# A hybrid Mamba-2/MLA trunk kernel: a planner that groups the scan's products of neighbouring chunks and knows the array's mode changes, x loaded in column halves, merged transposes, and more staged slices of the gated output

## The chip, the cores and the metric

The kernel runs on one core of a Trainium2 chip. A core has a matrix engine (TensorE, PE in the profile, with its weight loads as PEld), a vector engine (VectorE, DVE), a scalar engine (ScalarE, ACT), a general engine (GpSimd, POOL) and a sync engine (SyncE, SP) that here issues nearly all DMAs. Each engine takes its own instructions strictly in the order in which the program lists them. Engines wait for each other by semaphores. The metric is the device time of one launch in microseconds (us).

## What is computed

The reference is a trunk of two layers on x of 2048 tokens by 1024 features, all in float32: a Mamba-2 mixer, then multi-head latent attention (MLA), each behind an RMSNorm and with a residual add, and a last RMSNorm.

```python
def mamba2_mixer(h, w_in, conv_w, conv_b, dt_bias, A_log, D_skip, g_out, w_out):
    proj = h @ w_in                                  # z, x B C, dt
    xBC = silu(causal_depthwise_conv(xBC, conv_w, conv_b))
    dt = softplus(dt_raw + dt_bias)
    y = ssd_chunked_scan(xh, dt, A, B, C)            # 32 heads of 64, 4 groups, state 128
    y = (y + D_skip * xh) * silu(z)
    y = group_rms(y) * g_out                         # 4 groups of 512 channels
    return y @ w_out

def step(state, inp):                                # one chunk of the scan
    y_intra = einsum(C B^T, L, dt, x)                # L = exp(cum_t - cum_s), causal
    y_inter = einsum(C, state, exp(cum))
    new_state = state * exp(cum_end) + einsum(B, w_end, x)

def mla_shared_kv(h, ...):                           # 256 latents + 32 rotary
    ckv = rms_norm(rms_norm(h) @ w_dkv)
    kv = ckv @ w_ukv                                 # k and v of 16 heads of 64

def mla_mixer(h, k_nope, k_rope, v, ...):
    cq, gate = split(h @ w_in)                       # 384 latents, 1024 gates
    q = rms_norm(cq) @ w_uq
    o = causal_block_attention(q, k, v)              # 16 heads, 2048 tokens
    return (o * silu(gate)) @ w_out
```

The output is `rms_norm(h, g_final)` after both residuals.

## The kernel before

**Stages.** The 2048 tokens are four blocks b of 512, each kept as four row tiles of 128 by 1024. The stages and their stretches in the profiled execution are: the layers part, which holds Mamba (to about 1400 us) and the MLA projections (to about 1930 us); the attention (to about 2600 us); and `back()`, the output projection with the final norm (to the end).

**Mamba.** There are 16 items (b, g): a token block and one of the four groups of heads. For each item `xbc` and `zgate` make the projections of a group (products of the split weights `wsp` with the transposed x, `xT`), `ssd` runs the scan, and `outp` projects the gated result back. The loop in `mamba` (L1448) interleaves the scan of one item with the projections of the next. Most products are three passes over split operands (a high and a low half).

A block begins with `load_x` (L1547: four loads of 128 by 1024 floats, the tiles `hx`, and the rows' mean squares on ACT, written into `yt`), then `prep`, which transposes the tiles on PE into `ps` banks and splits each bank into the high half of `xT` on ACT and the low half on DVE, and `steps`, which works out dt and its running sums in small tiles named `big` and `d_dt` on DVE. The constants lie in one tile, `pack`: an identity matrix in its first 128 columns, then masks and vectors.

**The scan of a chunk.** An item has four chunks c of 128 tokens, so there are 64 in all. `decays` (L1798) loads the row of running sums broadcast into a tile `big` of 128 by 8 by 128 (ring of two buffers), and turns it on ACT (eight Relu of 128 by 128, one Exp of 128 by 1024) and DVE (a product with the tile `CB`) into the decay matrix E. `inputs` makes `Xd` (x times dt) and others. In `ssd` (L1847) the chunk's inner product is 16 matmuls, for eight heads and two halves of the chunk, each with 64 output rows and 64 columns, into the bank `yi`:

```python
for h in range(8):
    hc = slice(h * 64, (h + 1) * 64)
    for t in (slice(0, 64), slice(64, P)):
        nc.tensor.matmul(yi[t, hc], E[:, h, t], Xd[:, hc], start=True, stop=True)
```

Nearly all other matmuls of the layers part use 128 output rows. In the profile each of these 16 leaves two records (`ps<-Xd,big 128*64 128x64`), so 32 records to a chunk.

**Who sets the order.** In the layers part no engine is called directly. The class `Score` (L523) records every instruction with the buffers it uses. `cost` (L570) gives each an issue time and a latency in ns, `graph` (L630) works out who must wait for whom, and `plan` (L832) repeats two passes PLANS times: `forward` (L698) is a list scheduler that simulates the five engines and the DMA and always takes the ready instruction of highest rank, and `backward` (L780) gives new ranks as the time left to the end; rings of buffers are handed out in the order in which their tiles started. The best of the plans is kept and `play` (L875) writes it out, so every instruction of the layers part carries the line L878.

**MLA.** `mla_kv_down` and `mla_cq` make the latents; `turned` (L2062) scales each of four row tiles, splits it into a float16 pair and transposes it with DMAs on SP: one DMA for each row tile and each 128 latents, so 8 for the keys' latents and 12 for the queries' in a block. The results `yT` and `BC` are the operands of the up-projections.

**Attention.** Its order comes from the class `Pace`, a simulation of its own with fixed tables. Within it, slices k of block 0's gated output are staged for `back()`: task G loads the attention's output, the gate and a row of scales into a staging tile `os` (L2251, L2254), H multiplies them (L2260, L2262), I and J split the product into a float16 pair (L2324, L2327). GATED is the number of staging tiles, and ASKED says behind which of the last heads each slice is asked for.

**back().** For each block, 8 slices k are the contraction of the output projection: `gated` (L2459) loads the three parts into `os` (three buffers), gates them on DVE, makes the high half `oT` on ACT (L2466) and the low half on DVE (L2467), and PE adds the three products into eight banks. `residual` (L2479) adds the banks into the row tiles `h`; `final` (L2483) norms them on DVE (L2487) and stores them. This part is ordered by the tile framework, close to the order of the code.

## Time and profile before

The profile is one execution; the other figures are device times of runs of the kernel.

| what | us |
| --- | --- |
| median of 3 runs | 2784.39 |
| lowest and highest of the runs | 2779.01 and 2787.86 |
| the profiled execution's own time | 2791.74 |
| its span, first to last instruction | 2789.9 |
| time around the span | 1.8 |
| mean granted TensorE clock | 0.994 |

A row of the windows view gives a stretch, the busy time and the count of instructions of each engine in it, the granted clock as a share of full speed, the share of the DMA engines' time, and GB/s. A row of the lines view is a group of instructions: its line, engine and operation, the tiles out<-in, the shapes (for matmuls first the rows of the stationary operand by its columns), the count, the busy time and the mean of one in ns, and the engine's idle time just ahead of them with what ended it. A row of the timeline has the start, the length, the engine and the operation, and in brackets the idle time before it and what ended that. Busy times of two engines overlap, so they do not add up to the span. The kernel before has its layers part on L878; the changed kernel has it on L907.

### The profile page before, as it was taken

How to read it: one execution, taken by the hardware profiler on the slowest of the kernel's cores; microseconds unless marked ns; L12 is line 12 of the kernel's file. 1: busy time of each engine (PE TensorE's matmuls, PEld its weight loads, DVE VectorE, ACT ScalarE, POOL GpSimd, SP SyncE). 2: the span in 40 equal slices, each digit the busy share in tenths (PEclk: the TensorE clock that was granted, in tenths of full speed). 3: DMA queues.
4: the chain of work that ended last, by engine and by line, in shares of the span. 5: the costliest groups of instructions: out<-in, count | busy, mean ns of one | idle time of the engine just before them, and what ended most of it. 6: DMA issues, size and time to landing. Idle time of an engine off the chain costs nothing. (4 is left out here: it accounts for less than half of the span.)

```text
span 2789.9 us, 48569 instructions
## 1 busy us (share of the span) xinstructions
PE 2737.9 (98%) x16120; PEld 1550.7 (56%) x16120; DVE 2220.0 (80%) x5048; ACT 1864.2 (67%) x4914; POOL 675.6 (24%) x832
## 2 busy tenths in 40 slices
PE   7999999999999999999999999999999999999998
PEld 6888766554555555555555545454555555555443
DVE  5889899999988879888786564646889888889676
ACT  6889877877776667666655453334888888888322
POOL 0000000000000000000002121324888888888200
PEclk9999999999999999999999999999999999999999
DMA  5333456768668655586567987976999999999894
GB/s 178 98 113 105 118 178 220 215 204 256 187 187 256 175 141 178 160 243 185 145 186 232 292 236 210 250 197 183 181 189 183 186 203 198 190 200 185 209 278 153
DMA packets 687904, 535.88 MB, mean 192 GB/s; under 512 B 496642, under 2 KB 538626, under 8 KB 687652
## 3 DMA queue, kind: packets, MB, share of 16 engines
q1 hardware_dynamic: 674500, 490.16, 69.4%
q0 software_dynamic: 13152, 42.61, 5.1%
q8 instruction: 127, 2.08, 0.3%
q14 instruction: 125, 1.02, 0.1%
HBM read 307.57 MB, written 108.66 MB: 149 GB/s over the span
## 5 line engine op out<-in xcount | busy, mean ns | idle before, releaser
L878 PE MATMUL ps<-xT,wsp 128*128 128x512 f16 (+2 forms) x2416 | 567.7, 386 | 8.7 <-DVE wsp L878 6.0
L878 PE MATMUL ps<-wsp,xT 128*128 128x512 f16 (+3 forms) x2304 | 464.4, 358 | 1.9 <-DVE Sp L878 1.2
L2356 ACT ACTIVATE Pr<-ps,nm 128x512 f32<-128x512 f32 (+3 forms) x640 | 394.5, 628 | 83.7 <-DVE nm L2351 78.1
L2345 DVE TENSOR_REDUCE mx<-ps 128x1 f32<-128x512 f32 (+3 forms) x640 | 366.4, 604 | 54.1 <-PE ps L2311 45.9
L878 PEld LDWEIGHTS <-wsp 128*128 128x128 f16 x2448 | 234.0, 98 | 281.2 <-issue 21.6
L2362 POOL TENSOR_TENSOR HL<-Pr,HL 128x512 f16<-128x512 f32 x320 | 372.6, 1164 | 25.6
L878 PE MATMUL ps<-wsp,yT 128*128 128x512 f16 (+1 forms) x1536 | 356.7, 385 | 1.0 <-DVE rb L878 0.6
L878 POOL DMA_DIRECT2D gate_d<-xs x24 | 13.8, 590 | 1115.4 <-DVE kn L878 1101.3
L878 PEld LDWEIGHTS <-xT 128*128 128x128 f16 x1920 | 185.7, 98 | 166.5 <-issue 6.2
L904 PE MATMUL ps<-K,xT 96*128 96x512 f16 (+3 forms) x640 | 223.0, 348 | 2.9 <-ACT Pr L2356 1.8
L906 PE MATMUL ps<-K,xT 96*128 96x512 f16 (+3 forms) x640 | 221.9, 347 | 0.0
L905 PE MATMUL ps<-K,xT 96*128 96x512 f16 (+3 forms) x640 | 221.8, 347 | 0.0
L2361 POOL CAST HL<-Pr 128x512 f16<-128x512 f32 x320 | 196.6, 614 | 91.7 <-ACT Pr L2356 91.5
L878 DVE SCALAR_TENSOR_TENSOR cacc<-craw,pack,cacc 128x512 f32<-128x512 f32 x288 | 211.4, 746 | 4.6 <-ACT cacc L878 4.1
L878 PEld LDWEIGHTS <-yT 128*128 128x128 f16 x1152 | 110.2, 98 | 129.2 <-issue 3.8
L878 ACT ACTIVATE big<-big,d_cum 128x128 f32<-128x128 f32 x512 | 168.5, 393 | 8.8 <-DMA big<-cumT 8.8
L878 PE MATMUL ps<-xT,st 128*128 128x512 f16 x672 | 154.8, 382 | 3.7 <-DMA st<-w_d 3.7
L2375 ACT ACTIVATE PH<-ps 128x512 f16<-128x512 f32 (+3 forms) x320 | 143.4, 484 | 14.1 <-PE ps L2370 13.3
L2397 PE MATMUL ps<-PX,xT 128*64 128x512 f16 (+1 forms) x640 | 146.2, 383 | 1.6 <-DMA PX<-HL 1.2
L2397 PEld LDWEIGHTS <-xT 128*128 128x128 f16 (+1 forms) x1280 | 95.4, 103 | 91.4 <-issue 15.4
L2356 ACT ACTIVATION_READ_ACCUMULATOR Pr<-ps,nm 128x1 f32 x640 | 133.8, 209 | 0.0
L2370 PE MATMUL ps<-pack,Pr 128*128 128x128 f32 x896 | 133.4, 274 | 0.3 <-ACT Pr L2356 0.3
(380 smaller groups left out, 5348.3 us busy)
## 6 DMA issues: line engine op xcount, KB each, us to landing
wsp<-w_d SPq DMA_DIRECT2D x68, 512.0 KB, 3.9
wraw<-in_ssm_w_in_dram SPq DMA_DIRECT2D x128, 256.0 KB, 3.2
big<-cumT SPq DMA_DIRECT2D x64, 512.0 KB, 4.2
wraw<-in_ssm_w_out_dram SPq DMA_DIRECT2D x64, 256.0 KB, 3.3
w_d<-wsp SPq DMA_DIRECT2D x32, 512.0 KB, 4.3
wsp<-wo_d SPq DMA_DIRECT2D x32, 512.0 KB, 4.3
st<-w_d SPq DMA_DIRECT2D x56, 256.0 KB, 3.7
wsp<-wu_d SPq DMA_DIRECT2D x28, 512.0 KB, 4.2
```

Source lines behind the costliest of these rows:

```text
L878: call(*[self.real(x) for x in args], **{k: self.real(x) for k, x in named.items()})
L904: mm(out, l_hi, r_hi, start=start, stop=False)
L905: mm(out, l_hi, r_lo, start=False, stop=False)
L906: mm(out, l_lo, r_hi, start=False, stop=stop)
L2345: v.tensor_reduce(m[:, at:at + 1], s, AX.X, ALU.max, negate=True)
L2356: nc.scalar.activation(tile("Pr", n, j, c)[:, :w], bank("S", n, j, c)[:, :w], AF.Exp, bias=moves[(4 * n + j) % len(moves)], accum_out=sums ...
L2361: nc.gpsimd.tensor_copy(u[:, 0], x)
L2362: nc.gpsimd.tensor_tensor(u[:, 1], x, u[:, 0], ALU.subtract)
L2370: nc.tensor.transpose(bank("T", n, k)[:, j * P:(j + 1) * P], tile("Pr", n, j, k // 4)[:, k % 4 * P:(k % 4 + 1) * P], self.ident)
L2375: nc.scalar.activation(tile("PH", n, k)[:, c], bank("T", n, k)[:, c], AF.Copy)
L2397: nc.tensor.matmul(o, weights, half(n, k, low), start=start, stop=not left[n][at[0]])
```

## The change

It has six parts.

1. The planner's model: DMAs get an issue time, a latency and a time on the wires (`wires`); an SP instruction may not be planned more than EARLY (30 us) ahead of its due time; PLANS goes from 12 to 16; a matmul with 64 output rows and at least 64 columns belongs to `half`, a change between `half` and the rest costs TURN (119 or 94 ns) in `forward`, and PE stays among the `half` ones while one is ready.
2. Pairs: `parts` names the 16 matmuls of each chunk. The first chunk's 16 of a pair (c = 0 or 2) also get the second chunk's needs from other engines, and both banks keep neighbouring places in the ring, so that both groups can be planned as one of 32.
3. The start: `pack` is loaded in two DMAs, the identity first; x of block 0 in column halves, eight loads in place of four; `links` put the first four half loads ahead of the rest of `pack` and the four square passes on ACT behind the fourth split of `xT`.
4. `turned`: one DMA for up to 256 latents, so 4 in place of 8 and 8 in place of 12 in a block.
5. The staging of gated slices in the attention: four sets in place of two (two of them in places whose tiles are done with), another ASKED, and a delay of 7500 in place of 5500 ns in the simulation.
6. `back()`: five buffers of `os` in place of three.

```diff
-GATED = 2
-ASKED = {61: (0,), 62: (1,), 63: (2, 3, 4, 5, 6)}
+GATED = 4
+ASKED = {62: (0, 1), 63: (2, 3, 4, 5, 6)}
...
-                self.at(self.now + 5500, lambda k: self.ready["DVE"].append(("H", k, 0)), k)
+                self.at(self.now + 7500, lambda k: self.ready["DVE"].append(("H", k, 0)), k)
...
-PLANS = 12
+PLANS = 16
+EARLY = 30000
...
             if named.get("transpose"):
-                return 1400, 3300
-            issue = 700 if engine == "POOL" else 400
-            return issue, -moved
+                self.wires[len(self.ops)] = 545 + moved / 288
+                return 1300, 2470 + moved / 276
+            self.wires[len(self.ops)] = 102 + moved / 359
+            return 700 if engine == "POOL" else 400, 2000 + moved / 276
...
+            if out.shape[0] == 64 and n >= 64:
+                self.half.add(len(self.ops))
...
+        for m, n in self.links:
+            if all(m != k for k, _ in preds[n]):
+                preds[n].append((m, False))
+        for (b, g, c), part in self.parts.items():
+            if c % 2 == 0:
+                needs = {m for n in self.parts[b, g, c + 1] for m, _ in preds[n] if ops[m][0] != "PE"}
+                for n in part:
+                    preds[n] += [(m, True) for m in needs]
...
+    TURN = 119, 94
...
-        est = [0.0] * len(ops)
+        est = [max(0.0, due + rank[n] - EARLY) if o[0] == "SP" else 0.0 for n, o in enumerate(ops)]
...
-                heapq.heappush(r, (rank[n], n))
+                heapq.heappush(ready["half"] if n in self.half else r, (rank[n], n))
+            if e == "PE" and ready["half"] and (mode or not r or ready["half"][0] < r[0]):
+                r = ready["half"]
...
+            if e == "PE" and mode != (n in self.half):
+                mode = not mode
+                t += self.TURN[mode]
...
-                order = sorted(self.owns, key=lambda o: (min(start[n] for n in o.ops), o.first))
+                at = {id(o): (min(start[n] for n in o.ops), o.first) for o in self.owns}
+                for (b, g, c), part in self.parts.items():
+                    if c % 2:
+                        pair = [ops[x[0]][4][0].own for x in (self.parts[b, g, c - 1], part)]
+                        at[id(pair[1])] = at[id(pair[0])]
+                order = sorted(self.owns, key=lambda o: at[id(o)])
...
-        nc.sync.dma_start(self.pack, self.a["c_pack"])
+        for cs in (slice(0, P), slice(P, PACK)):
+            nc.sync.dma_start(self.pack[:, cs], self.a["c_pack"][:, cs])
+        ops = self.score.ops
         self.load_x(0, self.a["x"][0:TB])
+        self.score.links += [(0, n) for n in range(2, 6)] + [(n, 1) for n in range(2, 6)]
+        squares = [n for n, o in enumerate(ops) if o[0] == "ACT"][:4]
...
+            if n == 0:
+                turned = [n for n in range(at, len(ops)) if ops[n][0] == "ACT"]
+                self.score.links += [(turned[3], n) for n in squares]
...
-        for i in range(4):
-            nc.sync.dma_start(xs[i], src[i * P:(i + 1) * P, :])
+        n = 1 if b else 2
+        for h in range(n):
+            cs = slice(h * D // n, (h + 1) * D // n)
+            for i in range(4):
+                nc.sync.dma_start(xs[i][:, cs], src[i * P:(i + 1) * P, cs])
...
+            self.score.parts[b, g, c] = range(at, len(self.score.ops))
...
-            for k in range(n):
-                nc.sync.dma_start(out[k][:, i], u[:, k].rearrange("p s c -> p (s c)"), transpose=True)
+            for k, m, o in sets:
+                nc.sync.dma_start(o[:, i], u[:, k:k + m].rearrange("p k s c -> p (k s c)"), transpose=True)
...
-            self.staged = [self.t(self.wo, f"os{k}", [P, 3, TB], bufs=1) for k in range(GATED)]
+            staged = [self.t(self.wo, f"os{k}", [P, 3, TB], bufs=1) for k in range(2)]
...
+            self.staged = staged + [free[0:3], free[4:7]]
...
-                s = self.t(sp, "os", [P, 3, TB], bufs=3)
+                s = self.t(sp, "os", [P, 3, TB], bufs=5)
```

How the instructions move at three places follows; a row is an instruction, or several alike, as the program lists them for one engine, and a number behind a tile's name tells buffers apart.

On PE, at the first two chunks of item (0, 3), before: the bank of the first chunk is `ps_3893`, written by products of `Xd` and `big`.

```order
L878 MATMUL ps_3851<-xT_3677,wraw_3834 64x512
L878 MATMUL ps_3847<-wsp_3740,yT_3792 128x512 x2
L878 MATMUL ps_3893<-Xd_3766,big_3349 64x64 x12
L878 MATMUL ps_3909<-pack,yt_3891 128x128 x4
L878 MATMUL ps_3893<-Xd_3766,big_3349 64x64 x4
L878 MATMUL ps_3925<-Xp_3828,Bt_3614 128x512 x2
L878 MATMUL ps_3818<-wsp_3756,yT_3680 128x512
```

The same place in the changed kernel; the banks of the two chunks are `ps_4446` and `ps_4471`.

```order
L907 LDWEIGHTS wsp_4259
L907 MATMUL ps_4371<-xT_3683,wsp_4259 128x512
L907 MATMUL ps_4446<-Xd_3759,big_3779 64x64 x16
L907 MATMUL ps_4471<-Xd_4059,big_4344 64x64 x16
L907 MATMUL ps_4496<-Sp_4251,Ct_3770 128x512 x3
L907 MATMUL ps_4505<-pack,xs_3274 128x128
L907 MATMUL ps_4505<-pack,xs_3377 128x128
```

Two runs of 12 and 4, with the next chunk's products elsewhere, have become one run of 32. Over the layers part PE changes between matmuls of 64 and of 128 output rows 164 times before and 78 times now, so it goes into the 64-row mode and back 82 and 39 times; the number of matmuls is the same, and in the attention it is 96 changes in both.

On ACT at the start of the program, before: the squares of the four x tiles are the writes of `yt` and `ms`, and `wsp` is the first split weight, that of dt.

```order
L878 ACTIVATE pack<-pack 128x32
L878 ACTIVATE yt_171,ms_172<-hx_139 128x1024
L878 ACTIVATE yt_191,ms_172<-hx_148 128x1024
L878 ACTIVATE yt_208,ms_172<-hx_150 128x1024
L878 ACTIVATE yt_216,ms_172<-hx_152 128x1024
L878 ACTIVATE xT_230<-ps_174,pack 128x512
L878 ACTIVATE xT_240<-ps_176,pack 128x512
L878 ACTIVATE wsp_243<-wraw_154 128x8x32
```

The same place in the changed kernel; `wsp_227` is the first split weight of B and C.

```order
L907 ACTIVATE xT_187<-ps_162,pack 128x512
L907 ACTIVATE xT_193<-ps_164,pack 128x512
L907 ACTIVATE wsp_196<-wraw_155 128x8x32
L907 ACTIVATE pack<-pack 128x32
L907 ACTIVATE xT_187<-ps_166,pack 128x512
L907 ACTIVATE xT_193<-ps_168,pack 128x512
L907 ACTIVATE yt_220,ms_221<-hx_139 128x1024
L907 ACTIVATE wsp_227,nrm<-wraw_160 128x256
```

Four splits of `xT` and the first weight now stand ahead of the first square pass, and weight splits stand between the square passes. On SP, eight loads of 512 KB (four `hs`, four `hx` of the next block), which stood between the third and the fourth weight load, now stand behind many more weights, and the second halves of x stand among the first weights; on DVE, the dt chain, about 20 instructions on `big`, stood ahead of the weight splits and is now mixed with them.

On DVE in `back()`, at the turn from block 0 to block 1, before: `oT_29928` and `oT_29938` are the low halves of the seventh and eighth slice of block 1, and the writes of `h` are block 0's final norm.

```order
L2467 TENSOR_TENSOR oT_29877<-os_29870,oT_29877 128x512
L1338 SCALAR_TENSOR_TENSOR rsy_4128_29911<-rsq_4127_29909,rsy_4125_29905 128x4
L2487 SCALAR_TENSOR_TENSOR h_29804<-h_29804,rsy_4128_29911,gf 128x1024
L2487 SCALAR_TENSOR_TENSOR h_29805<-h_29805,rsy_4128_29911,gf 128x1024
L2487 SCALAR_TENSOR_TENSOR h_29806<-h_29806,rsy_4128_29911,gf 128x1024
L2487 SCALAR_TENSOR_TENSOR h_29807<-h_29807,rsy_4128_29911,gf 128x1024
L2260 TENSOR_TENSOR os_29921<-os_29921 128x512
L2260 TENSOR_TENSOR os_29931<-os_29931 128x512
L2262 SCALAR_TENSOR_TENSOR os_29921<-os_29921,us 128x512
L2262 SCALAR_TENSOR_TENSOR os_29931<-os_29931,us 128x512
L2467 TENSOR_TENSOR oT_29928<-os_29921,oT_29928 128x512
L2467 TENSOR_TENSOR oT_29938<-os_29931,oT_29938 128x512
```

The same place in the changed kernel; `oT_29903` is the eighth slice of block 1, and `os_30118` is the first of block 2.

```order
L2303 TENSOR_TENSOR os_29896<-os_29896 128x512
L1365 SCALAR_TENSOR_TENSOR rsq_4119_29874<-rsx_4109_29854,rss_4118_29872 128x4
L2305 SCALAR_TENSOR_TENSOR os_29896<-os_29896,us 128x512
L1367 SCALAR_TENSOR_TENSOR rsy_4120_29876<-rsq_4119_29874,rsy_4117_29870 128x4
L2534 SCALAR_TENSOR_TENSOR h_29769<-h_29769,rsy_4120_29876,gf 128x1024
L2534 SCALAR_TENSOR_TENSOR h_29770<-h_29770,rsy_4120_29876,gf 128x1024
L2534 SCALAR_TENSOR_TENSOR h_29771<-h_29771,rsy_4120_29876,gf 128x1024
L2534 SCALAR_TENSOR_TENSOR h_29772<-h_29772,rsy_4120_29876,gf 128x1024
L2514 TENSOR_TENSOR oT_29903<-os_29896,oT_29903 128x512
L2303 TENSOR_TENSOR os_30118<-os_30118 128x512
L2305 SCALAR_TENSOR_TENSOR os_30118<-os_30118,us 128x512
L2514 TENSOR_TENSOR oT_30125<-os_30118,oT_30125 128x512
```

Before, the gating of the seventh and eighth slice stood behind the four writes of `h`; now the seventh stands wholly ahead of them, and of the eighth only the low half, one instruction, stands behind.

More of the change, by code (lines that the diff above doesn't have):

```diff
@@ L525, in __init__ @@
     def __init__(self, nc, blank, name):
-        self.ops, self.owns, self.rings = [], [], {}
+        self.ops, self.owns, self.rings, self.wires, self.links = [], [], {}, {}, []
+        self.half, self.parts = set(), {}
         self.blank, self.name = blank, name
@@ L705, in forward @@
         waiting = {e: [] for e in ENGINES}
-        ready = {e: [] for e in ENGINES}
+        ready = {e: [] for e in ENGINES + ("half",)}
+        mode = False
         events = [(0.0, e) for e in ENGINES]
@@ L760, in forward @@
                 free[e] = t + step
-            if took < 0:
-                dma = max(dma, t) - took / 260
-                took = max(dma, t + 1900 - took / 160) - t + self.LATE
+            if n in self.wires:
+                dma = max(dma, t + 500) + self.wires[n]
+                took = max(took, dma + 1690 - t) + self.LATE
             if e == "SP":
@@ L838, in plan @@
         order = sorted(self.owns, key=lambda o: o.first)
-        best = None
+        best, due = None, 0.0
         for i in range(PLANS):
-            made = self.forward(rank, order)
+            made = self.forward(rank, order, due)
             if made is None:
@@ L2060, in latent, with turned @@
         return raw, f
-    def turned(self, raw, f, n, tag):
+    def turned(self, raw, f, n):
         nc = self.nc
-        out = [self.t(self.sp, tag, [P, 4, 2, P], F16, bufs=4) for _ in range(n)]
+        sets = [(k, m, self.t(self.sp, "yT" if m == 2 else "BC", [P, 4, 2 * m, P], F16, bufs=4))
+                for k, m in ((0, 2), (2, 1))[:n - 1]]
         for i, x in enumerate(raw):
```

37 lines of the change are left out of this document (23 added, 14 removed).

## The prediction

> **What bounds the kernel now.** I read the page's busy times first, then the windows by stage, then PE's lines and timeline in the stages where it idles.
>
> ```profile
> span 2789.9 us, 48569 instructions
> PE 2737.9 (98%) x16120; PEld 1550.7 (56%) x16120; DVE 2220.0 (80%) x5048; ACT 1864.2 (67%) x4914; POOL 675.6 (24%) x832
> 0.00:70.00 70.00, 54.66 (x230) 42.41 (x230) 39.44 (x105) 44.33 (x119) 0.20 (x4) 0.93 0.55 179
> 70.00:1400.00 1330.00, 1329.40 (x7998) 780.22 (x7997) 1159.85 (x2486) 975.73 (x2569) 0.70 (x1) 1.00 0.62 177
> 1400.00:1930.00 530.00, 516.24 (x2757) 263.58 (x2756) 305.22 (x704) 234.38 (x467) 115.88 (x170) 0.99 0.79 226
> 1930.00:2600.00 670.00, 664.83 (x4338) 386.68 (x4337) 594.09 (x1521) 566.35 (x1680) 551.70 (x652) 1.00 1.01 189
> 2600.00:2790.00 190.00, 172.81 (x806) 77.85 (x804) 121.37 (x236) 43.38 (x82) 7.07 (x7) 0.97 0.73 216
> ```
>
> PE is the bound: 52 of 2789.9 us are idle. Its idle time by stage is 70 − 54.66 = 15.3 at the start, 0.6 in the whole scan, 13.8 in the MLA projections, 5.2 in the attention and 17.2 in the tail, of which some is the work behind the last matmul. So time can go in two ways: from idle and half-clock time outside the scan, or, within the scan, from what the array itself takes, since there no wait is left to remove.
>
> **Changes of the array's mode (part 2, with the planner).** This is PE's timeline around one chunk's products:
>
> ```profile
> 414.63 1.89 PE L878 MATMUL ps<-xT,wsp 128*128 128x512 f16 x8
> 416.36 0.27 PE L878 MATMUL ps<-pack,BC 128*128 128x128 f32 x1
> ...
> 416.79 1.03 PE L878 MATMUL ps<-Xd,big 128*64 128x64 f32 x28
> 417.75 0.82 PE L878 MATMUL ps<-wsp,xT 128*128 128x512 f16 x3
> 418.50 0.34 PE L878 MATMUL ps<-Xd,big 128*64 128x64 f32 x4
> 418.77 0.39 PE L878 MATMUL ps<-wsp,xT 128*128 128x512 f16 x1
> ```
>
> From start to next start, 28 records took 417.75 − 416.79 = 0.96, and 4 records 418.77 − 418.50 = 0.27, with the same kind of product behind. So a record costs (0.96 − 0.27)/24 = 0.029, and a stay that returns at once costs 0.27 − 4 × 0.029 = 0.155 more than its records. The entry shows ahead of it: a product of 512 columns takes (416.36 − 414.63)/8 = 0.216, three take 0.65, and from 417.75 to 418.50 passed 0.75, so 0.10. A stay therefore costs about 0.26. The order has 82 stays before and 39 now, 43 fewer: 43 × 0.26 = 11. It is one place in the trace; the lower bound takes the entry alone, 4.4, the upper the 0.26 with a little more, 12. PE was busy 1329.40 of 1330 there, so I know of no idle time in which this could already be hidden. I take −11.
>
> **New waits in the scan (pairs, EARLY, other ranks).** A pair needs the inputs of two chunks at once, and PE takes its work in order, so a late E of the second chunk stops everything queued behind: the state products and the projections. The planner knows all of this only from its model, and the model's DMA and latency figures change in the same edit. Bounds: 0, as the 0.6 of idle shows what planned waits cost before, and 20, since the same planner leaves 13.8 in MLA's 530 us, at which rate the scan would idle 35, and a little over half of that is the most that I give to an edit of the ranks. I take +4, nearer the scan's own row. The one reason for a gain is better ranks, and with 0.6 of idle there is none to gain.
>
> **The start (part 3).** PE, ACT and the loads:
>
> ```profile
> 5.63 1.09 PE L878 MATMUL ps<-pack,hx 128*128 128x128 f32 x4 [5.63 <-DMA hx<-in_x_dram]
> ...
> 15.01 1.07 PE L878 MATMUL ps<-xT,wsp 128*64 128x512 f32 x3 [1.89 <-DVE wsp L878]
> ...
> 25.84 0.96 PE L878 MATMUL ps<-xT,wsp 128*128 128x512 f32 x3 [0.88 <-ACT wsp L878]
> 30.91 6.07 PE L878 MATMUL ps<-xT,wsp 128*128 128x512 f32 x15 [4.10 <-DVE wsp L878]
> ...
> 43.56 22.66 PE L878 MATMUL ps<-xT,wsp 128*128 128x512 f32 x96 [1.69 <-ACT wsp L878]
> ```
>
> ```profile
> 12.40 1.27 ACT L878 ACTIVATE xT<-ps,pack 128x512 fp32r<-128x512 f32 x2 [0.69 <-PE ps L878]
> ```
>
> ```profile
> L878 ACT ACTIVATE xT<-ps,pack 128x512 fp32r<-128x512 f32 x8 | 5.0, 702 | 0.7 <-PE ps L878 0.7
> L878 ACT ACTIVATE wsp<-wraw 128x256 fp32r<-128x256 f32 x13 | 5.0, 421 | 5.9 <-DMA wraw<-in_ssm_w_in_dram 5.9
> L878 ACT ACTIVATE yt<-hx 128x1024 bf16<-128x1024 f32 x4 | 4.2, 1057 | 2.6 <-DMA hx<-in_x_dram 2.6
> ```
>
> ```profile
> wraw<-in_ssm_w_in_dram SPq DMA_DIRECT2D x128, 256.0 KB, 3.2
> hx<-in_x_dram SPq DMA_DIRECT2D x16, 512.0 KB, 5.2
> ```
>
> ```profile
> 15.50:19.00 3.50, 3.34 (x9) 1.68 (x8) 3.50 (x8) 3.35 (x10) 0.00 (x0) 0.51 1.02 408
> 29.20:36.00 6.80, 5.09 (x12) 4.07 (x13) 3.97 (x15) 0.82 (x3) 0.00 (x0) 0.50 0.31 71
> ```
>
> The stage has 15.3 of idle and two stretches at half clock, which cost 0.49 × 3.34 + 0.50 × 5.09 = 4.2 more: 19.5. Three things go. A half of a tile (256 KB) lands in about 3.2 where a whole one takes 5.2; since the queue is shared I take 1.2 of the 2.0. The first split of `xT` at 12.40 waits behind the four squares (4.2); they now stand later. The waits of 0.88, 4.10 and 1.69 are for split weights that were queued behind other loads and behind the dt chain on DVE. What sets the pace then is ACT: 5.0 for xT, 4.2 for the squares, and 16 weight passes and their sums at about 0.5 each, 8: some 17 us from about 6.5, so the last weight is split near 25, where PE waited for the last one until 43.56. The first load still takes 4.4 of the 19.5, so at most 15 goes; at least 5 goes, if only the two middle waits (0.88 + 4.10) do. ACT keeps short gaps and the dt chain is itself later, so I take −12, nearer the upper end because the order shows all three moves. What is passed: five more DMAs on SP, and the loads of the next block move behind the weights; they are wanted only a block later, about 330 us on, so nothing is late for that.
>
> The Trainium skill, page "DMA: Bandwidth & Descriptors", section Bandwidth, says to batch DMAs to 1 MiB and more for 75% of peak, which speaks against halving 512 KB loads; the two rows (256 KB in 3.2, 512 KB in 5.2) agree that a byte costs more in the smaller one, and only the first landing counts here. [...]
>
> The half clock in 15.5 to 19.0 came behind an idle time of only 1.89, that in 29.2 to 36.0 behind one of 4.10. The Trainium skill, page "TensorE: Matmul & The Clock Gate", Part 1, has the clock fall after at least one idle window of about 3.4 us; the second row agrees and the first doesn't. By the page only the 2.5 us of the second would go with the waits, and the start's term would be −10.
>
> **MLA (part 4, and the planner).**
>
> ```profile
> 1568.60:1572.00 3.40, 3.40 (x9) 1.19 (x9) 3.40 (x7) 0.69 (x2) 2.65 (x4) 0.50 1.02 333
> 1800.70:1807.50 6.80, 5.82 (x14) 2.09 (x15) 6.10 (x13) 1.38 (x2) 2.02 (x4) 0.50 0.89 268
> ```
>
> ```profile
> L878 PE MATMUL ps<-xT,st 128*128 128x512 f16 x670 | 154.4, 382 | 3.7 <-DMA st<-w_d 3.7
> ...
> L878 PE MATMUL ps<-yT,wsp 128*128 128x512 f16 x432 | 101.3, 386 | 7.8 <-DVE yT L878 4.5 <-DVE big L878 2.7 <-DVE Xp L878 0.7
> ```
>
> ```profile
> 1554.49 10.62 SPq L878 DMA_TRANSPOSE xT<-wsp  x4
> ```
>
> ```profile
> 1565.55 0.88 DVE L878 TENSOR_SCALAR xT<-xT,xg 128x1024 f16<-128x1024 f16 x2 [5.80 <-DMA xT<-wsp]
> ```
>
> Of the idle 13.8, 3.7 is for a load and 4.5 for DVE, which itself sat 5.80 for a transpose; the two half-clock stretches cost (3.40 + 5.82)/2 = 4.6. So 18 is there. SP spent 10.62/4 = 2.7 on a transpose there; 32 of its transposes go, but the bytes stay, and the one that DVE waited for at 1565.55 isn't among them. In the order that rescaling stands 10 places behind the last weight split in place of 5, and one such pass takes 0.88/2 = 0.44, so 5 × 0.44 = 2.2 more is covered. I take −6: the 2.2, the half-clock stretch that follows the wait (3.40/2 = 1.7), and 2 of the 8 of idle that DVE and the load hold, from a plan that now counts a transpose's time on the wires. Bounds: −16, all but a remnant, and +6, if the new plan has another such wait as at 1565.55.
>
> **Attention and the tail (parts 5 and 6).**
>
> ```profile
> L904 PE MATMUL ps<-W,oT 128*128 128x512 f16 x192 | 73.5, 383 | 5.9 <-ACT oT L2466 5.9
> ...
> L906 PE MATMUL ps<-W,xT 128*128 128x512 f16 x16 | 6.1, 380 | 2.0 <-DVE xT L2327 2.0
> ```
>
> ```profile
> 2660.72 4.87 DVE L2487 SCALAR_TENSOR_TENSOR h<-h,rsy,gf 128x1024 f32<-128x1024 f32 x4
> ```
>
> ```profile
> 2667.49 1.29 ACT L2466 ACTIVATE oT<-os 128x512 f16<-128x512 f32 x2 [7.68 <-DVE os L2262]
> ```
>
> The 5.9 is PE's wait for `oT`, whose gating stands behind DVE's four norm passes (4.87): ACT sat 7.68 for it. With five `os` buffers the seventh slice is gated ahead of those passes, and of the eighth only the low half is behind. The 2.0 at the stage's start is for a staged slice; with four sets the slices are made earlier. So 7.9 is there; some comes back, as the eighth's low half still waits for up to 4.87, while the products of the seventh (24 of 0.216, 5.2) cover it. I take −5, bounds −2 (the staged slice alone) and −8 (all). In the attention, where PE is busy 664.83 of 670, the second asking one head earlier moves six SP loads and a few DVE passes; DVE's 594.09 of 670 hides them, and if it didn't they would cost a few tenths each.
>
> **The sum.** −11 + 4 − 12 − 6 − 5 = −30. Against the profiled execution, 2791.74 becomes 2762. That execution lies 7.4 above the median of the runs; the terms are differences, so from the median 2784.4 the forecast is **2754**.
>
> **The rivals.** *Pairs wait (slower).* The ring `big` has two buffers, and a pair holds both until its last product; then both E of the next pair must be loaded and made.
>
> ```profile
> big<-cumT SPq DMA_DIRECT2D x64, 512.0 KB, 4.2
> ```
>
> ```profile
> L878 ACT ACTIVATE big<-big,d_cum 128x128 f32<-128x128 f32 x512 | 168.5, 393 | 8.8 <-DMA big<-cumT 8.8
> ...
> L878 ACT ACTIVATE big<-big 128x1024 f32<-128x1024 f32 (+1 forms) x68 | 68.7, 1010 | 1.6 <-DVE big L878 1.4
> ```
>
> ```profile
> L878 DVE TENSOR_TENSOR big<-big,CB 128x1024 f32<-128x1024 f32 x64 | 77.9, 1219 | 0.9 <-ACT big L878 0.5
> ```
>
> That chain is 4.2 + 2 × (168.5/64 + 1.01) + 1.2 = 12.7, if nothing else stands between. A pair comes every 1330/32 = 41.6, so there are 29 to spare, and that is what speaks against it; for it, that ACT is busy 73% and DVE 87% there, so the chain is much longer than its own work. It decides from a mean wait of (2793 − 2750)/31 = 1.4 at each of 31 pairs; with 2 the time is 2754 − 4 + 62 = 2812. *DVE takes the bound.* With 1159.85 of 1330 busy, PE's gain in the scan runs into DVE's order: the 11 is given back as waits and the other terms stay, −12 − 6 − 5 and 8 of new waits: 2769. *MLA's waits all go*, −16 in place of −6: 2744. *The halves bring nothing*: eight loads end as late as four, the weights behind them too, and only the two middle waits go, −5 in place of −12 at the start: 2761. *The change does not do what it says:* the array's turn is no cost of its own, only what the next weight load takes anyway (0 in place of −11), the start brings 5, the tail 2, and MLA's new plan loses 6: 2787.
>
> **How the numbers follow.** Forecast 0.52; DVE 0.18; MLA 0.09; halves 0.09; nothing gained 0.08; pairs wait 0.04. A difference of 0.3%, 8.4 us, is about what a measurement of this kernel tells from no change: faster is below 2776, slower above 2793. The first four are faster, 0.88; the fifth the same, 0.08; the last slower, 0.04. The range reaches below to the forecast with MLA at its end and the start at 15 and a little more, 2754 − 10 − 3 − 5 = 2736, and above to the DVE rival with the start at its lower bound, 2769 + 5 = 2774; about 0.15 lies outside.
>
> **What would show it.** Right: the stretch of the scan shorter by 7 to 12 with PE's idle there under 8; records of `Xd,big` in runs of 64; the last wait for `wsp` before 35; the 5.9 at `oT` under 2. Wrong: idle at `Xd,big` released by `big` on DVE or ACT (pairs wait); PE's idle in the scan up by 10 spread over products released by DVE; PE's busy time in the scan unchanged with 43 stays fewer, which would end the mode's price; a new MLA wait of several us. A time above 2776 would make the prediction wrong.

## The result and the profile after

The changed kernel took 2742.93 us (median of 4 runs, 2740.09 to 2749.07), the kernel before 2785.11 beside it (2779.01 to 2787.86): a ratio of 0.985, 95% interval 0.983 to 0.987, so 42 us less. The forecast was 2754 with a range of 2736 to 2774. The two profiled executions lie further apart than the medians, 2789.9 − 2738.2 = 51.7 in their spans, since the one of before is 6.6 above its kernel's median and the one of after 2.8 below; the parts below are parts of the 51.7. Four executions, one each of `oldcost` and `plans28` below and two of the kernel before beside them, took 4028 to 4446 us at a granted clock of 0.59 to 0.65, and no ratio here counts them.

The page of the changed kernel, its first lines, and its windows up to 1930 us:

```profile
span 2738.2 us, 48514 instructions
PE 2710.9 (99%) x16120; PEld 1543.6 (56%) x16120; DVE 2212.3 (81%) x5048; ACT 1867.2 (68%) x4914; POOL 672.3 (25%) x832
```

```profile
0.00:70.00 70.00, 63.48 (x287) 50.24 (x288) 49.76 (x127) 53.99 (x147) 0.20 (x4) 1.00 0.49 137
70.00:1400.00 1330.00, 1329.27 (x8117) 781.53 (x8116) 1167.34 (x2523) 988.84 (x2595) 0.70 (x1) 1.00 0.63 182
1400.00:1930.00 530.00, 526.16 (x2852) 272.80 (x2850) 320.61 (x754) 252.15 (x525) 149.13 (x212) 1.00 0.84 235
```

PE's idle time fell from 52.0 to 27.3. In the first 70 us it is 6.5 where it was 15.3, in the scan 0.7 (it was 0.6), and in the 530 us that held the MLA projections 3.8 (it was 13.8). The granted clock is 1.00 in all three, where it was 0.93 and 0.99 in the first and the third.

Where the time went is seen from when the same work is reached. These are rows of the tile view, with the shortest, median and longest time in ns and the first and last start of a group; of before:

```profile
L878 PE MATMUL ps<-Xd,big x2048: 222/222/271, 92.1 to 1447.2; 128*64 128x64 f32 x187
L904 PE MATMUL ps<-K,xT x640: 218/378/631, 1930.6 to 2593.7; 96*128 96x512 f16 x128, 96*128 96x128 f16 x16, 96*128 96x384 f16 x16
L904 PE MATMUL ps<-W,oT x192: 379/379/634, 2648.4 to 2780.2; 128*128 128x512 f16 x192
```

and of after:

```profile
L907 PE MATMUL ps<-Xd,big x2048: 222/222/271, 82.2 to 1416.1; 128*64 128x64 f32 x187
L933 PE MATMUL ps<-K,xT x640: 219/378/390, 1887.6 to 2549.2; 96*128 96x512 f16 x128, 96*128 96x128 f16 x16, 96*128 96x384 f16 x16
L933 PE MATMUL ps<-W,oT x192: 379/379/379, 2605.1 to 2728.7; 128*128 128x512 f16 x192
```

The last product of the scan comes 31.1 earlier, the first of the attention 43.0, the last of the attention 44.5, the last of the output projection 51.5. So the start and the scan gained about 31, MLA 12, the attention 1.5 and the tail 7.

**The start.** From PE's timeline in the first 75 us, and ACT's first split:

```profile
3.96 1.08 PE L907 MATMUL ps<-pack,hx 128*128 128x128 f32 x4 [3.96 <-DMA hx<-in_x_dram]
...
9.46 0.66 PE L907 MATMUL ps<-pack,hx 128*128 128x128 f32 x4 [1.17 <-DMA hx<-in_x_dram]
...
18.60 4.45 PE L907 MATMUL ps<-xT,wsp 128*128 128x512 f32 x18 [0.75 <-ACT wsp L907]
...
24.75 22.18 PE L907 MATMUL ps<-xT,wsp 128*128 128x512 f32 x94
```

```profile
7.99 1.26 ACT L907 ACTIVATE xT<-ps,pack 128x512 fp32r<-128x512 f32 x2 [5.56 <-PE ps L907]
```

The first half of x is there 1.7 earlier, the first split 4.4 earlier, and after 18.60 PE waits for no weight; before, the last such wait ended at 43.56. Idle fell by 8.8, and the 4.2 of half clock are gone: 13.0.

**The scan.** A pair in the timeline:

```profile
406.64 2.09 PE L907 MATMUL ps<-Xd,big 128*64 128x64 f32 x64
408.65 2.98 PE L907 MATMUL ps<-wsp,xT 128*128 128x512 f16 x13
```

64 records, two chunks, in one stay of 2.01 from start to start, with no idle time ahead. Over the whole kernel the lines view has it so:

```profile
L907 PE MATMUL ps<-Xd,big 128*64 128x64 f32 x2048 | 66.9, 224 | 0.0
```

**MLA and the tail.** The waits for `yT` (4.46 at 1568.52) and for `st` (3.67 at 1801.68) have no counterpart; what is left is 1.86 and 0.68 for `BC`. In the tail PE never waits for `oT`: the longest of those products takes 379 ns where it was 634, so the half clock has gone as well. From the first of them to the last it is 123.6 where it was 131.8, so 8.2 less. Ahead of the first of them 1.2 was lost: PE now waits 2.40 for `PL` at 2558.46 and 1.63 for `PX` at 2565.13, while its 2.03 for `xT` at 2607.91 has gone.

### The profile page after: what moved, and what is told of

It reads as the page before. It is cut to its first block, busy times and chain, and to the rows that moved or that the text cites. A ratio compares the mean times of both kernels' runs of the same rounds, so it can differ in the third digit from the quotient of the medians.

```text
span 2738.2 us, 48514 instructions
## 1 busy us (share of the span) xinstructions
PE 2710.9 (99%) x16120; PEld 1543.6 (56%) x16120; DVE 2212.3 (81%) x5048; ACT 1867.2 (68%) x4914; POOL 672.3 (25%) x832
## 4 chain that ended last, share of the span: by engine, by line
PE 92%; DMA 3%; DVE 2%; ACT 1%; issue 1%; SPq 0%; POOL 0%; DVEq 0%; ACTq 0%
PE ps L907 64%; PE ps L2444 6%; PE ps L933 6%; PE ps L934 6%; PE ps L935 6%; PE ps L2417 3%; DMA xT<-wsp 1%; DVE mx L2392 1%; PE ps L2359 0%; DMA PX<-HL 0%; DMA h_d<-hs 0%; DMA yT<-yt 0%; DMA hs<-h_d 0%; ACT wsp L907 0%; DMA xT<-ri_d 0%
## 5 line engine op out<-in xcount | busy, mean ns | idle before, releaser
L907 PE MATMUL ps<-xT,wsp 128*128 128x512 f16 (+2 forms) x2416 | 559.9, 384 | 0.7 <-ACT wsp L907 0.7
L907 PE MATMUL ps<-wsp,yT 128*128 128x512 f16 (+1 forms) x1728 | 398.2, 384 | 0.0
L907 PEld LDWEIGHTS <-yT 128*128 128x128 f16 x1344 | 128.8, 98 | 150.7 <-issue 4.3
L907 ACT ACTIVATE Xw<-ps,d_wend 128x64 f32<-128x64 f32 x512 | 112.4, 326 | 43.0 <-DVE y L907 33.7
```

The costliest lines, as they stand in the source:

```text
L907: call(*[self.real(x) for x in args], **{k: self.real(x) for k, x in named.items()})
```

## The experiments

My theory after the result: four separate gains, each from the part to which the prediction gave it; modes 0.26 a stay, the start, MLA, the tail. The chief rival: the planner's other edits, not the parts named, brought the gains. The runs show each kernel's median beside the kernel before on the same chip (2785 to 2787 in all of them). Comparisons with the changed kernel go by its own median, 2742.93.

### Is a change of mode a cost of its own? Two splits of the runs

The plan of the changed kernel is kept; only the run of 32 is broken up before it is written out. With `split2` the second half goes behind one matmul more, with `split3` a matmul from ahead of the run is also put into it.

```diff
     def play(self):
+        self.part_runs(2)
         for n in sorted(range(len(self.ops)), key=lambda n: (self.start[n], n)):
...
+            run = sorted([*first, *self.parts[b, g, c + 1]], key=lambda n: at[n])
...
+            rest = [n for n in pe[i:i + 12] if n not in self.half][:pieces - 1]
...
+            for j in range(1, pieces):
+                for k, n in enumerate(run[size * j:size * j + size]):
+                    self.start[n] = self.start[rest[j - 1]] + 0.01 * (k + 1)
```

> The changed kernel with its plan kept, but in 31 of the pairs the second half of the run of 32 products is moved behind the one matmul that followed the run: 70 stays in the 64-row mode in place of 39, nothing else moved. Theory (each stay has a price of its own, 0.26 us): 31 x 0.26 = 8 us more than the changed kernel's 2743, so 2751, with no more idle time on PE in the scan. Rival (the turn costs nothing, what the scan gained came from the planner's other edits): 2743, within 2.

> As split2, and in nearly all pairs a matmul from ahead of the run is moved into it as well: 100 stays in place of 39. Theory: 61 x 0.26 = 16 us more than the changed kernel, so 2759, and twice the step of split2. Rival (no price of a turn): 2743, within 2; a rival in which only the first weight load behind a run costs would give about the entry's share less, 61 x 0.16 = 10, so 2753.

Measured: 2750.38 (2749.21 to 2752.29; ratio to before 0.987, 0.985 to 0.989) and 2759.30 (2758.42 to 2760.82; 0.990, 0.988 to 0.992). Against the changed kernel that is 7.5 for 31 stays, 0.24 each, and 16.4 for 61 stays, 0.27 each. The ratio of split2 alone still overlaps the changed kernel's (0.983 to 0.987); that of split3 doesn't, and with it the rival without a price is out, as is the one in which only the entry costs (2753). The tile view places it in the scan (split2, then split3):

```profile
L928 PE MATMUL ps<-Xd,big x2048: 222/222/271, 82.1 to 1424.5; 128*64 128x64 f32 x187
```

```profile
L929 PE MATMUL ps<-Xd,big x2048: 222/222/271, 82.4 to 1434.0; 128*64 128x64 f32 x187
```

The last product comes 8.4 and 17.9 later than after's 1416.1, with the scan's idle at 0.6 and 0.8 where it was 0.7. The timeline of split2 shows one break:

```profile
409.08 1.15 PE L928 MATMUL ps<-Xd,big 128*64 128x64 f32 x32
410.16 0.39 PE L928 MATMUL ps<-wsp,xT 128*128 128x512 f16 x1
410.48 1.15 PE L928 MATMUL ps<-Xd,big 128*64 128x64 f32 x32
411.56 2.76 PE L928 MATMUL ps<-wsp,xT 128*128 128x512 f16 x12
```

From start to start the halves take 1.08 each, 2.16 where the whole took 2.01: 0.15 for leaving once more. The product between takes 0.32 in place of 0.216: 0.10 for entering again. These are the two terms of the prediction, found at another place. The price doesn't show as idle time: PE is busy throughout.

### Pairs without the rest, and the rest without pairs

`onlypairs` is the kernel before with `half`, `parts` and TURN alone; `noturn` is the changed kernel without them.

The diff of noturn against the changed kernel:

```diff
-            self.score.parts[b, g, c] = range(at, len(self.score.ops))
...
-                self.half.add(len(self.ops))
+                pass
```

> The kernel before with only the pairs and the mode in its planner: 39 stays in place of 82, the start, the transposes, the model of the DMAs, the staging and the three buffers as before. Theory: 43 x 0.26 = 11 us less than before, 2774, with the idle times of the start (15), MLA (14) and the tail still there. Rival (the turn costs nothing): 2785. Rival (pairs make PE wait, which the new model of the DMAs then mended): above 2785, with idle time of PE ahead of the products.

> The changed kernel planned without knowledge of the mode and without pairs; the start, the merged transposes, the model of the DMAs, the staging and the five buffers stay. The plan has 87 stays. Theory: 48 stays x 0.26 = 12 us more than the changed kernel, 2755, all of it in the scan's stretch and none of it idle time. Rival (the planner's other edits brought what the scan gained): 2743, within 3.

Measured: onlypairs 2792.12 (2789.32 to 2799.09), ratio 1.0024, 1.0012 to 1.0036, so a little slower than before with 43 stays fewer. noturn 2767.92 (2765.73 to 2772.86), ratio 0.994, 0.992 to 0.995: 25 more than the changed kernel, twice what 48 stays cost.

The windows of onlypairs and PE's lines in its scan:

```profile
70.00:1400.00 1330.00, 1321.99 (x7991) 778.03 (x7990) 1160.78 (x2489) 980.44 (x2577) 0.70 (x1) 1.00 0.61 178
1400.00:1930.00 530.00, 515.16 (x2763) 263.64 (x2764) 305.14 (x707) 230.69 (x457) 117.01 (x171) 0.99 0.80 225
```

```profile
L898 PE MATMUL ps<-wsp,xT 128*128 128x512 f16 (+1 forms) x1491 | 344.1, 385 | 3.1 <-DVE wsp L898 2.7 <-ACT wsp L898 0.4
...
L898 PE MATMUL ps<-Sp,Ct 128*128 128x512 f32 x168 | 57.4, 445 | 2.0 <-ACT craw L898 2.0
```

The scan idles 8.0 where it idled 0.6, and the waits are not ahead of the pairs' own products but at weight splits and state products that DVE and ACT now bring too late. Two stretches behind such waits (1.97 at 417.05 and 2.66 at 512.98) also run at half clock, which costs 3.4 more:

```profile
418.43:421.84 3.41, 3.41 (x10) 1.21 (x9) 3.41 (x7) 3.41 (x12) 0.00 (x0) 0.50 0.28 77
514.00:517.41 3.41, 3.41 (x11) 1.49 (x9) 3.41 (x7) 2.76 (x8) 0.00 (x0) 0.50 0.64 177
```

So 7.4 of idle and 3.4 of half clock, nearly all of the 11, are handed back within the scan. This is the prediction's rival on DVE, in a kernel planned with the old model. The spans of the two profiled executions, 2789.4 and 2789.9, are alike; why the median is 6 above before's isn't settled.

In noturn the scan is without any idle, and PE's lines from 1400 to 1940 have this:

```profile
L907 PE MATMUL ps<-xT,st 128*128 128x512 f16 x672 | 157.7, 386 | 14.4 <-DMA st<-w_d 14.4
```

```profile
1628.02 5.20 SPq L907 DMA_TRANSPOSE xT<-wsp  x1
1633.31 3.49 SPq L907 DMA_DIRECT2D st<-w_d  x2
...
1638.88 9.10 SPq L907 DMA_TRANSPOSE xT<-wsp  x2
```

The 14.4 are two waits for loads in MLA, 5.25 at 1646.51 and 9.14 at 1792.80. The first load stands in SP's queue among transposing DMAs of `xT`, which the edit doesn't touch and which hold SP for 4.6 to 5.2 us each here. The clock was at half around both waits (from 1645.14 to 1651.97 and from 1788.50 to 1798.74), which cost 5.7. With 48 stays, 12, that makes 32, about the distance of the two profiled executions (2771.0 − 2738.2 = 32.8). The medians lie 25 apart; noturn's profiled execution is 5 above its own. So a new plan costs or saves 10 us and more in MLA, whatever it was made for: this confounds each run that plans anew.

### The transposes in MLA, and the planner's model of the DMAs

`turnold` undoes the merging alone; `oldcost` gives the changed kernel the old issue times, latencies and allowances; `noearly` takes EARLY out.

First turnold, then noearly, then the core of oldcost, each against the changed kernel:

```diff
-        sets = [(k, m, self.t(self.sp, "yT" if m == 2 else "BC", [P, 4, 2 * m, P], F16, bufs=4))
-                for k, m in ((0, 2), (2, 1))[:n - 1]]
+        sets = [(k, 1, self.t(self.sp, "BC" if n == 2 else "yT", [P, 4, 2, P], F16, bufs=4)) for k in range(n)]
```

```diff
-        est = [max(0.0, due + rank[n] - EARLY) if o[0] == "SP" else 0.0 for n, o in enumerate(ops)]
+        est = [0.0] * len(ops)
```

```diff
-            self.wires[len(self.ops)] = 102 + moved / 359
-            return 700 if engine == "POOL" else 400, 2000 + moved / 276
+            issue = 700 if engine == "POOL" else 400
+            return issue, -moved
```

> The changed kernel with a transposing DMA for each 128 latents as before, 32 more of them in the MLA projections. Theory (merging them took PE's waits in MLA away): idle of PE there back from 4 to 10 or more, 6 to 10 us more than 2743, so 2750. Rival (the planner's model of the DMAs did it, and it places 32 more transposes as well): 2743, within 2.

> The changed kernel planned with the old model of the DMAs (issue, latency, allowance); EARLY, pairs, mode, merged transposes, start and staging stay. It fills the fourth place beside new model and merged (idle in MLA 3.8), new model and not merged (24), old model and not merged (14 to 15). Theory (merging the transposes ends MLA's waits, the model has to fit the transposes of the plan): idle in MLA about 4 to 6 and PE's idle in the scan below 2, so 2743 to 2747. Rival (the new model is what keeps MLA and the pairs supplied): 10 of idle or more in MLA and 8 in the scan as in the run with only the pairs, so 2758 or more.

> The changed kernel without EARLY: an SP instruction may be planned as far ahead as its buffers allow. Theory (EARLY keeps far loads from standing ahead of those that are needed, at the start above all): idle at the start back to 10 or so, some 4 more than 2743, so 2747. Rival (ranks alone keep the order): 2743, within 3, or a shift either way from another plan alone.

Measured: turnold 2770.22 (2768.34 to 2778.53; 0.994, 0.993 to 0.996), 27 more than the changed kernel. Its last scan product is at 1418.5, 2.4 later than after's; its first attention product at 1916.4, 28.8 later. PE's lines there, and SP's queue just ahead of the longest wait, 8.19 for a load of `wsp` at 1556.40:

```profile
L907 PE MATMUL ps<-wsp,xT 128*128 128x288 f16 (+1 forms) x768 | 116.5, 317 | 17.9 <-DMA wsp<-w_d 10.9 <-DVE xT L907 7.0
```

```profile
1531.21 9.75 SPq L907 DMA_TRANSPOSE xT<-wsp  x2
...
1543.72 7.98 SPq L907 DMA_DIRECT2D wsp<-w_d  x3
```

The load stands behind two transposes of `xT` that take 9.75 together, and the edit doesn't touch those. The merged ones cost SP no more than single ones (tile view of the MLA projections, before from 1460 us and after from 1440 us, then `xT` in after):

```profile
L878 SPq DMA_TRANSPOSE yT<-yt x48: 1167/1244/2858, 1500.6 to 1871.2; - x48
```

```profile
L907 SPq DMA_TRANSPOSE yT<-yt x32: 1188/1201/1957, 1456.8 to 1824.6; - x32
L907 SPq DMA_TRANSPOSE xT<-wsp x24: 1238/1706/5280, 1495.4 to 1753.5; - x24
```

Those of `yT` in after carry two sets of 128 latents where before's carry one, and the median is about the same. So 32 fewer are 32 × 1.24 = 40 us of SP. Those of `xT` carry four times as much as before's `yT`, and take 1.7 in the median and up to 5.3.

oldcost: 2771.40 (2762.34 to 2786.80, a wide spread); ratio 0.995, 0.993 to 0.997. Its windows, from the execution of 2786.80, the longest of them:

```profile
70.00:1400.00 1330.00, 1319.38 (x7987) 775.88 (x7986) 1158.14 (x2489) 979.53 (x2578) 0.70 (x1) 1.00 0.61 180
1400.00:1930.00 530.00, 506.81 (x2703) 258.55 (x2702) 295.97 (x680) 221.67 (x440) 114.84 (x168) 0.97 0.80 224
```

10.6 of idle in the scan and 23.2 in MLA, of which some may be that execution's own, since it took 15 more than the median. The median alone is 13 above the rival's 2758, so the theory (merging is enough) is out and the rival fits. The four places of the table of MLA's idle are then (onlypairs also lacks EARLY and the new start):

| | one DMA for 128 latents | merged |
| --- | --- | --- |
| old model | 14.8 (onlypairs) | 23.2 (oldcost) |
| new model | 24.0 (turnold) | 3.8 (after) |

In these four plans neither edit alone is worth anything, and both together 11. But other plans with both edits idle 5.3 (plans28), 8.1 (noearly), 10.6 (startold) and 17.7 (noturn), so part of this is the luck of a plan, and the runs can't separate it further. SP's time alone isn't it: between the last scan product and the first of the attention, the transposes held SP for 167 us before, 121 in after and 179 in turnold, but for only 116 in oldcost, which idles about as much as turnold.

noearly: 2762.65 (2760.05 to 2764.89; 0.992, 0.990 to 0.993), 20 more, not 4. Its windows and its SP queue at the start:

```profile
0.00:70.00 70.00, 60.20 (x261) 45.56 (x262) 46.80 (x118) 50.19 (x135) 0.20 (x4) 0.98 0.60 192
70.00:1400.00 1330.00, 1322.72 (x8010) 778.10 (x8008) 1163.72 (x2501) 985.48 (x2586) 0.70 (x1) 1.00 0.61 179
1400.00:1930.00 530.00, 521.89 (x2831) 268.81 (x2831) 314.53 (x734) 241.22 (x485) 129.13 (x188) 1.00 0.80 225
```

```profile
7.60 3.38 SPq L907 DMA_DIRECT2D hs<-in_x_dram  x4
...
15.23 16.09 SPq L907 DMA_DIRECT2D wraw<-in_ssm_w_in_dram  x7
```

The next block's loads stand ahead of most of the weights again, as expected (idle at the start 9.8 in place of 6.5), but the larger part is 7.3 of idle in the scan (0.7 in after) and 8.1 in MLA (3.8). Whether EARLY itself prevents these or another plan brought them, as the rival has it, this run can't tell.

### The start

```diff
-        for cs in (slice(0, P), slice(P, PACK)):
-            nc.sync.dma_start(self.pack[:, cs], self.a["c_pack"][:, cs])
+        nc.sync.dma_start(self.pack, self.a["c_pack"])
...
-        n = 1 if b else 2
+        n = 1
```

(with the links taken out.)

> The changed kernel with the start as before: pack in one load, x in whole tiles, no links; all else stays. Theory (the start's gain comes from these): PE's idle in the first 70 us back from 6.5 to about 15 and half clock with it, 12 more than the changed kernel's 2743, so 2755. Rival (the planner's new model of the DMAs alone moves the weights ahead of the next block's loads): 3 to 5 more, for the first load and the squares alone, 2747.

Measured: 2755.41 (2753.03 to 2756.17; 0.988, 0.987 to 0.990), 12.5 more, the theory's number. The tile view says otherwise:

```profile
L907 PE MATMUL ps<-Xd,big x2048: 222/222/271, 86.9 to 1421.8; 128*64 128x64 f32 x187
L933 PE MATMUL ps<-K,xT x640: 216/378/390, 1903.1 to 2564.2; 96*128 96x512 f16 x128, 96*128 96x128 f16 x16, 96*128 96x384 f16 x16
```

The first scan product is 4.7 later than after's, the last 5.7, the first of the attention 15.5. So 5 belongs to the start, and 10 arose in MLA, where the new plan idles 10.6. The rival's 3 to 5 is about right for the start itself, and the median agreed with the theory by chance.

### The staging and the five buffers

os3, then gated2:

```diff
-                s = self.t(sp, "os", [P, 3, TB], bufs=5)
+                s = self.t(sp, "os", [P, 3, TB], bufs=3)
```

```diff
-GATED = 4
-ASKED = {62: (0, 1), 63: (2, 3, 4, 5, 6)}
+GATED = 2
+ASKED = {61: (0,), 62: (1,), 63: (2, 3, 4, 5, 6)}
```

gated2 undoes the three edits of the staging together, the old delay of 5500 included; `beforestaged` is the kernel before with four sets, the new ASKED and 7500, and three buffers.

> The changed kernel with three buffers of os in back() in place of five. Theory (the fourth and fifth buffer let the seventh slice be gated ahead of the four norm passes): PE's 5.9 of idle at oT comes back with some half clock, 6 more than 2743, so 2749. Rival (the order of the staged slices, or the earlier start of the stage, took the wait away): 2743, within 1.

> The changed kernel with two staging sets, the old list of askings and the delay of 5500 in the attention. Theory: PE's 2.0 of idle at xT at the start of the last stage comes back, 2 more than 2743, so 2745. Rival (four sets cost the attention as much as they save behind it): 2743 or less.

> The kernel before with the staging of the attention alone changed: four sets, the new list of askings, the delay of 7500; three buffers of os, and all the rest as before. Theory (after the run with three buffers lost nothing: the staging alone ends the tail's waits): idle at oT 5.9 and at xT 2.0 gone, 8 us less than before, 2778. Rival (it takes the staging and the five buffers together): 2 less, 2784, with the 5.9 still there.

Measured: os3 2742.78 (2740.60 to 2743.79), no difference from the changed kernel's 2742.93; gated2 2748.82 (2745.26 to 2751.84), 6 more; beforestaged 2781.39, ratio 0.998, 0.997 to 0.999, so 5 less than before (3 to 8) where the theory had 8. PE's lines in the tail, of gated2 and of beforestaged:

```profile
L933 PE MATMUL ps<-W,oT 128*128 128x512 f16 x192 | 73.5, 383 | 3.4 <-ACT oT L2513 3.4
L935 PE MATMUL ps<-W,oT 128*128 128x512 f16 x192 | 73.3, 382 | 0.8 <-DVE oT L2514 0.7
L935 PE MATMUL ps<-W,xT 128*128 128x512 f16 x16 | 6.1, 380 | 1.3 <-DVE xT L2374 1.3
```

```profile
L906 PE MATMUL ps<-W,oT 128*128 128x512 f16 x192 | 72.8, 379 | 1.9 <-DVE oT L2471 1.9
```

With five buffers and two sets the waits are back; with four sets and three buffers nearly all are gone. DVE in gated2 has its four norm passes (4.87) ahead of the seventh and eighth slice again:

```profile
2616.22 4.87 DVE L2534 SCALAR_TENSOR_TENSOR h<-h,rsy,gf 128x1024 f32<-128x1024 f32 x4
2621.00 1.29 DVE L2303 TENSOR_TENSOR os<-os 128x512 f32<-128x512 f32 x2
```

In beforestaged, with three buffers, what comes first behind them is the low half of a slice that was gated ahead of them, as in the changed kernel:

```profile
2654.09 4.87 DVE L2491 SCALAR_TENSOR_TENSOR h<-h,rsy,gf 128x1024 f32<-128x1024 f32 x4
2658.88 0.68 DVE L2471 TENSOR_TENSOR oT<-os,oT 128x512 f16<-128x512 f32 x1
```

So the order at that place, which the prediction put down to the buffers, comes from the staging. By which of its three edits and which step of the framework's ordering it does so wasn't tried.

### More iterations of the planner

`plans28` changes PLANS from 16 to 28.

> The changed kernel with 28 iterations of the planner in place of 16, of which it keeps the plan that it believes the shortest. Theory (the model's best plan is also the chip's): 2740, 1 to 5 less. Rival (what differs from plan to plan lies in waits that the model does not see): 2743 to 2755, with idle in MLA above the changed kernel's 3.8.

Measured: 2741.96, ratio 0.984, 0.983 to 0.985, against the changed kernel's 0.985: the same, so neither the theory's gain nor the rival's loss shows. Its idle in MLA's window is 5.3. None of the runs beats the changed kernel clearly.

## Why the prediction came out as it did

- *Modes, −11:* right, in size and in mechanism. In the traces all stays of `Xd,big`, each from its first start to the next product's, take 71.7 before and 64.7 after; with 0.10 for each of 43 entries fewer that is 11 less. Added by hand, stays cost 0.24 to 0.27 each.
- *New waits in the scan, +4:* not there, 0.7 for 0.6. But the danger was real: plans of the same pairs with the old model idle 8.0 and 10.6. The prediction took the model of the DMAs as a risk; in oldcost, where it alone is undone, the scan's waits come back.
- *Start, −12:* 13.0 measured. The steps weigh otherwise than I put them: halves, split pack and links are 5 of it; that the weights come ahead of the next block's loads is the planner's doing, and EARLY has a part in it. The rival that the halves bring nothing is out: the first of them came 1.7 earlier.
- *MLA, −6:* mis-sized, and the largest error: 10.0 of idle and 4.6 of half clock went, 14.6 in PE's time (12 by the markers, perhaps because some work stood on the other side of the last scan product). The term gave only 2 of the 8 of idle at DVE and the load to the new plan, because "32 of its transposes go, but the bytes stay, and the one that DVE waited for at 1565.55 isn't among them". That the waited one isn't among them is right, and yet both waits went. What took them is open: SP was rid of 32 × 1.24, and undoing the merging alone brings 24.0 of idle, but oldcost, with the merging, idles 23.2. The prediction also took 2.7 of SP's time for a transpose from a row of `xT`, where those that go cost 1.24. The rival "MLA's waits all go" (−16) was the nearer one, and with it the sum is 2744.
- *Tail, −5:* 7 measured, or 8.5 with the attention's 1.5, just past the bound of −8: 8.2 at `oT`, its 6.2 of idle and 1.5 of half clock, less 1.2 that was lost ahead of it. The step "with five `os` buffers the seventh slice is gated ahead of those passes" failed: the five buffers are worth nothing, the staging all, so the size came out nearly right from the wrong part of the change.
- *The slower rival:* no pair waited for its E in the changed kernel, where PE's idle ahead of `Xd,big` is 0.0.
- *The half clock:* all three stages' stretches went with the waits, the one behind 1.89 of idle included. By the page "TensorE: Matmul & The Clock Gate" of the Trainium skill, Part 1, only those behind about 3.4 of idle were to be had. The traces don't bear this out, and the length of a wait alone doesn't decide either. Behind 1.86 at 2698.48 in gated2 the clock was 0.50, behind 1.86 at 1469.45 in after it was 1.00, and so it was behind 2.40 at 2558.46 there. What does decide is open. The stretches of gated2 and of after behind the 1.86 (the third number from the end is the clock):

```profile
2699.62:2703.04 3.42, 3.42 (x10) 1.18 (x9) 3.25 (x9) 0.72 (x2) 0.00 (x0) 0.50 0.00 0
```

```profile
1469.45:1476.30 6.85, 6.85 (x32) 3.13 (x33) 4.30 (x7) 3.43 (x6) 2.05 (x3) 1.00 0.73 207
```

Start, modes and MLA make 39 of the 43 up to the attention; 4 I can't place.

## What to carry to other kernels

An engine that reads as 100% busy can still hold time: count how often it changes its mode, price one change between two rows of a timeline, and group the work. When a planner gets a new constraint, look at its model of the queues in the same step; the constraint alone was worth nothing here. When a planner makes a new plan for each experiment, compare markers of the work in the trace and not medians, or break up one finished plan by hand: a median can agree with a theory by a wait that arose elsewhere.

## What was not expected of the hardware

A transposing DMA on SP held the queue for a median 1.24 us with 128 latents and 1.20 with 256. Those of `xT`, of 512 columns and their low halves, held it for 1.7 in the median and in crowded stretches for up to about 5 (5.20 for one, 9.10 and 9.75 for two). A stay of 64-row products among 128-row ones cost PE about 0.25 us, 0.10 on the way in and 0.15 on the way out, and showed as busy time. Waits of the same length, 1.86, were followed by half clock in one run and by full clock in another.
